# A hybrid DeltaNet/gMLP step: the first block begun behind two of four modulation quarters, their sums in column groups, x normed ahead of the halo rows

## The chip, the cores and the metric

The kernel runs on one core of a Trainium2 chip. The metric is device time in microseconds (us). Engines by their names in the profile: PE (TensorE matmul), PEld (its weight loads), DVE (VectorE), ACT (ScalarE), POOL (GpSimd) and SP, whose queue issues all DMAs of this kernel.

## The reference

One layer of a hybrid backbone for 128 context tokens and 2048 latent tokens of width 1024: an RMSNorm with a modulation computed from the conditioning vectors, a mixer (gated DeltaNet in two directions beside a gated spatial MLP, from one input projection), and a squared-ReLU MLP, each added to the residual.

```python
def modulation(cond, w_mod_l, b_mod_l):
    m = jax.nn.silu(cond) @ w_mod_l + b_mod_l
    return jnp.split(m[:, None, :], N_MOD, axis=-1)
...
    sh1, sc1, ga1, sh2, sc2, ga2 = mod
    h = rmsnorm(x, norm_mix_l) * (1.0 + sc1) + sh1
    o, s_new = mixer(h, s0, ...)
...
    proj = h @ w_in_l
    qkv = jax.nn.silu(centred_conv(qkv, conv_l))
```

Everything is float32. The change lies in the computation of `sh1` and `sc1`, of `h`, and of the first columns of `proj`, for the first 384 tokens.

## The kernel before

Tokens come as 17 tiles of 128 rows; tile 0 is the context. The first part works in six blocks, the first of tiles 0 to 2 (`BLOCKS`). For a block, `prep_block` makes eight *keys* `kH`, `kL` (one for each 128 of the 1024 features): features on partitions, tokens along the row, split in a rounded float32r part and its rest. In the first block a key is made from x normed by rows: three transposes on PE (a *turn*), the modulation by tables `a1`, `b1` on ACT into `full`, the split on DVE. A key has padding columns: zeros at the ends of a sequence, and *halo* columns, single neighbouring tokens needed by the convolution, which POOL casts from `halH` and `halL`; these come from ten halo rows `xh`, normed and transposed ahead. In the first block that is one column, 387.

`feature_tile` projects a block on 128 output features: for each key three matmuls (`mm3`: high by high, high by low, low by high), 24 in a group, into one PSUM buffer (`pj`, three of them, or `pt`), and then `convolve`, `to_tokens`, `to_features` and `products`. Group 1 (`gi` 1) are the k features, 0 the q, 2 the v, four tiles each. Weights come by 256 KB tiles (`raw_w`) and are split by `split_w`: a cast on ACT (`wH`), a difference on DVE (`wL`). `ab_block` projects the 16 gate columns.

The tables need four quarters of the modulation, each a product of the conditioning (two columns) with 1024 x 512 weights: m0 (shift, features 0 to 511), m1 (scale, the same features), m2 and m3 (shift and scale of features 512 to 1023). `mod_load` loads eight tiles, `mod_sum` sums them on PE in one row block of two partitions, `mod_out` transposes the row of sums and writes half a table. Keys 0 to 3 need m0 and m1, keys 4 to 7 also m2 and m3. The code issues m0, m1, m2, the halo rows, x, m3, the first four k weight tiles, and later twelve more; it emits the four sums ahead of the projections, in the order r0, r1, r2, r3. Then it runs keys 0 to 3 against three k feature tiles, makes keys 4 to 7, and goes on in the main loop, where each feature tile's steps are mixed with side work (`interleave`): weight splits of the next groups, modulation steps for the later parts of the layer (`MOD_STEPS` tells how many at each tile of the first block), the loads and keys of the next block.

Engine orders are made by a scheduler that simulates the program and takes, on each engine, what is ready first by order of emission, unless a dependence without a semaphore (`add_manual_dep` with `NoSync`) fixes the order. `WARM` is eight products of ones that PE runs at the very start. The pool `wp` has 49 places for tiles of 128 x 512, in which raw and split weights lie.

Of the kernel before, what the change touches and what calls it, by code (L numbers as in the profile page):

```python
# [8 lines left out]
F32 = mybir.dt.float32  # L9
# [31 lines left out]
MOD_STEPS = (1, 1, 0, 0, 0, 1, 0, 2, 0, 1, 1, 2)  # L41
# [23 lines left out]
def hybrid_step(  # L65
# [63 lines left out]
    def make_masks():  # L129

        one16 = wp.tile([P, P], F16, tag="w", name="one16")
        V.memset(one16, 1.0)
        bd = {}
        for w in (2, 4, 8, 16, 32, 64):
            m = bd2 if w == 2 else wp.tile([P, P], F16, tag="w", name=f"bd{w}")
# [159 lines left out]
    with ExitStack() as ph:  # L295
# [47 lines left out]

        def mod_load(half, c0):
            return [raw_w(w_mod[0, k * P : (k + 1) * P, c0 + half * 512 : c0 + half * 512 + 512])
                    for k in range(KT)]

        def mod_sum(raws, psum):

            pm = psum()  # L350
            for k in range(KT):
                T.matmul(pm[0:2, :], scond[:, k, :], raws[k], start=k == 0, stop=k == KT - 1)
            row = pf.tile([2, 512], F32, tag="first", name="first", bufs=2)
            A.copy(row, pm[0:2, :])
            return row

        def mod_out(row, half, dst, bias, scaled):

            pc = pm1()
            for i in range(4):  # L360
                T.transpose(pc[:, 2 * i : 2 * i + 2], row[:, i * P : (i + 1) * P], ident[0:2, 0:2])
# [9 lines left out]
        def split_mod_steps(jc):  # L371
# [3 lines left out]
            def fetch(k):  # L375
                u["raw", k] = pf.tile([P, 512], F32, tag="mraw", name="raw", bufs=2)
                load(out=u["raw", k], in_=w_mod[0, k * P : (k + 1) * P, jc * 512 : (jc + 1) * 512])

# [17 lines left out]

        m0 = mod_load(0, 0)
# [4 lines left out]
        r1 = mod_sum(m1, pj)  # L402
        m2 = mod_load(1, 0)
        mod_out(r0, 0, b1, vec[:, 0:8], False)

        make_masks()


        xh = pf.tile([P, D], F32, tag="xh", name="xh", bufs=1)[0:10, :]
        for m in range(5):  # L410
            load(out=xh[2 * m : 2 * m + 2, :], in_=x_sample[0, 255 + 384 * m : 257 + 384 * m, :])
        r2 = mod_sum(m2, pj)
# [8 lines left out]
        xs0 = []  # L421
        for t in BLOCKS[0]:
            x = p1.tile([P, D], F32, tag="x", name="x", bufs=3)
            load(out=x, in_=xrow(t))
            xs0.append(x)
        for x in xs0:
            norm_rows(x)

        def load_w1(gi, ks):
            return [w1_raw(gi, k) for k in ks]  # L430

        def w1_raw(gi, k):
            return raw_w(w_in[0, k * P : (k + 1) * P, gi * 512 : (gi + 1) * 512])
# [3 lines left out]
        def first_half(half):  # L437
            for k in range(half * 4, half * 4 + 4):
                V.tensor_scalar(out=hal[:, k, :], in0=hal[:, k, :], scalar1=a1[:, 1, k : k + 1],
                                scalar2=b1[:, 1, k : k + 1], op0=ALU.mult, op1=ALU.add)  # L440
            ks = slice(half * 4, half * 4 + 4)
            V.tensor_copy(halH[:, ks, :], hal[:, ks, :])
            V.tensor_tensor(out=halL[:, ks, :], in0=hal[:, ks, :], in1=f32(halH)[:, ks, :], op=ALU.subtract)

        def prep_block(bi):
# [49 lines left out]
            if bi == 0:  # L495
                zc, hc = [0, 129, 130], [(387, 1)]
            elif bi == 5:
                zc, hc = [n + 1], [(0, 8)]
            else:
                hc = [(0, 2 * bi - 2), (n + 1, 2 * bi + 1)]  # L500
            def column(k):
                full = p1.tile([P, 384], F32, tag="full", name="full", bufs=2)
                kH = p1.tile([P, 388], F32R, tag="h", name="kH", bufs=24)
                kL = p1.tile([P, 388], F32R, tag="h", name="kL", bufs=24)
# [6 lines left out]
                if bi == 0:  # L511
                    ps = pt()
                    for i, x in enumerate(xs):
                        T.transpose(ps[:, i * P : (i + 1) * P], x[:, k * P : (k + 1) * P], ident)
# [23 lines left out]
            blk = (hH, hL, ncol, segs)  # L538
# [5 lines left out]
        def feature_tile(blk, bi, gi, h):  # L544

            hH, hL, ncol, segs = blk
# [7 lines left out]
            def project(k):  # L554
                if k == 0:
                    u["ps"] = (pt if bi == 0 and j == 6 else pj)()
# [80 lines left out]
        def ab_block(blk, bi):  # L637
            hH, hL, ncol, segs = blk
# [3 lines left out]
            def project():  # L642
                ps = (pj if bi else pm1)()
                for k in range(KT):
                    T.matmul(ps[:, :ncol], abW[:, k, :], hH[k][:, :ncol], start=k == 0, stop=False)
                    T.matmul(ps[:, :ncol], abW[:, k, :], hL[k][:, :ncol], start=False, stop=k == KT - 1)
                for s, o, m, _ in segs:
# [116 lines left out]
        m3 = mod_load(1, D)  # L764
        wr = load_w1(1, range(4))
        mod_out(r1, 0, a1, vec[:, 8:16], True)
        r3 = mod_sum(m3, pm1)
        mod_out(r2, 1, b1, vec[:, 0:8], False)
        W1[1] += [split_w(r) for r in wr]
        first_half(0)  # L770
        abr = p1.tile([P, KT, 16], F32, tag="abr", name="abr", bufs=1)
        load(out=abr, in_=w_ab)
        wk = load_w1(1, range(4, KT))
        wr = load_w1(0, range(KT))
# [5 lines left out]
        mod_out(r3, 1, a1, vec[:, 8:16], True)  # L780
        W1[1] += [split_w(r) for r in wk]
        first_half(1)
        for k in range(4, KT):
            cols[k]()
        V.tensor_copy(abW[:, :, 0:16], abr)
        V.tensor_tensor(out=abW[:, :, 16:32], in0=abr, in1=f32(abW)[:, :, 0:16], op=ALU.subtract)
        wq = [lambda r=r: W1[0].append(split_w(r)) for r in wr]
        wv = [lambda k=k: W1[2].append(load_split(w_in[0, k * P : (k + 1) * P, 1024:1536])) for k in range(KT)]
# [3 lines left out]
        for bi in range(len(BLOCKS)):  # L792
            nxt = prep_block(bi + 1) if bi + 1 < len(BLOCKS) else None
            if bi == 0:
                order = [(1, 0), (1, 1), (1, 2), (0, 0), (0, 1), (1, 3), (0, 2), (0, 3)]
# [5 lines left out]
            for n, (gi, h) in enumerate(order):  # L801
                u = us[n] if bi == 0 and n < 3 else feature_tile(blk, bi, gi, h)
                tile_of[gi, h] = u
                main = u["main"][4:] if bi == 0 and n < 3 else u["main"]
# [1266 lines left out]
```

## Time and profile before

| what | us |
|---|---|
| runs | 2574.28, 2577.04, 2578.62 (median 2577.04) |
| profiled execution, its own time | 2580.59 |
| span of the profiled execution | 2578.7 |
| PE busy | 2539.4 |
| DVE busy | 1836.7 |
| ACT busy | 1259.7 |
| first projection matmul (line 241) | 36.20 |

In the lines of the profile a time stands in us from the span's start, followed by how long the row took, the engine, the line of the kernel, the operation, its output and inputs by the program's names, and in brackets the engine's idle time before it with what released it. A float32 matmul is two instructions there. Matmul ends are modelled, so starts are the better measure. The mean granted clock of the run is 0.997.

### The profile page before, as it was taken

What the parts mean: (1) busy time and instruction counts of PE and PEld (TensorE: products, weight loads), DVE (VectorE), ACT (ScalarE), POOL (GpSimd) and SP (SyncE); (2) the same over time, 40 slices, a digit from 0 to 9 for tenths busy, and PEclk for the clock granted to TensorE, in tenths of its full rate; (3) what the DMA queues carried; (4) which work ended last, traced back from release to release, by engine and by line L of the source; (5) the groups of instructions that cost most, each with busy time, mean ns of one, the idle gap of its engine ahead of it and who ended that gap; (6) DMA issues with size and microseconds to landing.
All of it is one profiled execution on the core that took longest, in us unless ns stands there. A gap on an engine that the chain in (4) does not pass through costs nothing.

```text
span 2578.7 us, 44496 instructions
## 1 busy us (share of the span) xinstructions
PE 2539.4 (98%) x15268; PEld 2139.2 (83%) x15268; DVE 1836.7 (71%) x3790; ACT 1259.7 (49%) x3119; POOL 234.2 (9%) x448
## 2 busy tenths in 40 slices
PE   9999999999999999999999999999999999999998
PEld 5999999788888787778888888888888888888887
DVE  5867757776677878886677876777675557685875
ACT  4755556555555667764355543544442433243442
POOL 3112212111111111210000000000000000000000
PEclk9999999999999999999999999999999999999999
DMA  8967737644454657885768789666579979786683
GB/s 293 307 209 216 209 111 256 225 158 153 145 156 159 214 165 243 277 274 176 281 204 257 231 270 358 194 181 188 148 248 370 331 273 330 259 259 205 221 264 113
DMA packets 503912, 588.66 MB, mean 228 GB/s; under 512 B 36148, under 2 KB 298588, under 8 KB 500102
## 3 DMA queue, kind: packets, MB, share of 16 engines
q1 hardware_dynamic: 503686, 585.82, 69.6%
q8 instruction: 120, 1.97, 0.3%
q14 instruction: 106, 0.87, 0.1%
HBM read 406.01 MB, written 179.67 MB: 227 GB/s over the span
## 4 chain that ended last, share of the span: by engine, by line
PE 89%; DMA 5%; DVE 4%; ACT 1%; issue 1%; POOL 0%; SPq 0%; POOLq 0%; DVEq 0%; ACTq 0%
PE f L241 17%; PE f L242 17%; PE f L243 17%; PE pj L241 7%; PE pj L243 7%; PE pj L242 7%; PE pd L1010 5%; PE pm L241 1%; PE pm L243 1%; PE pm L242 1%; DMA raw<-in_w_mod_dram 1%; PE pt L625 1%; PE pt L584 1%; PE pd L1093 1%; DMA hop_d<-opL 1%
## 5 line engine op out<-in xcount | busy, mean ns | idle before, releaser
L241 PE MATMUL f<-hop,zH 128*128 128x512 f32 (+1 forms) x976 | 376.2, 386 | 1.2 <-ACT zH L1531 1.2
L242 PE MATMUL f<-hop,zH 128*128 128x512 f32 (+1 forms) x976 | 376.1, 386 | 0.0
L243 PE MATMUL f<-hop,zL 128*128 128x512 f32 (+1 forms) x976 | 376.1, 386 | 0.0
L241 PE MATMUL f<-hop,wH 128*128 128x512 f32 x896 | 349.7, 391 | 0.6 <-ACT p L1604 0.6
L242 PE MATMUL f<-hop,wH 128*128 128x512 f32 x896 | 348.7, 389 | 0.0
L243 PE MATMUL f<-hop,wL 128*128 128x512 f32 x896 | 347.5, 389 | 0.0
L1531 ACT CAST zH<-zraw 128x512 fp32r<-128x512 f32 x240 | 146.9, 620 | 302.4 <-DMA zraw<-s_d 93.6
L241 PEld LDWEIGHTS f<-hop,zH 128*128 128x128 f32 x976 | 183.3, 188 | 38.6 <-ACT zH L1531 1.6
L243 PEld LDWEIGHTS f<-hop,zL 128*128 128x128 f32 x976 | 183.3, 188 | 37.3 <-DVE zL L1525 0.4
L242 PEld LDWEIGHTS f<-hop,zH 128*128 128x128 f32 x976 | 183.3, 188 | 36.9 <-issue 0.2
L1525 DVE TENSOR_TENSOR zL<-zraw,zH 128x512 fp32r<-128x512 f32 x240 | 163.2, 687 | 66.5 <-ACT zH L1531 54.0
L241 PEld LDWEIGHTS f<-hop,wH 128*128 128x128 f32 x896 | 168.2, 188 | 36.5 <-ACT p L1604 1.7
L243 PEld LDWEIGHTS f<-hop,wL 128*128 128x128 f32 x896 | 168.2, 188 | 35.3
L242 PEld LDWEIGHTS f<-hop,wH 128*128 128x128 f32 x896 | 168.3, 188 | 34.5
L241 PE MATMUL pj<-kH,wH 128*128 128x386 f32 (+2 forms) x568 | 190.5, 338 | 1.3 <-ACT junk L601 1.1
L243 PE MATMUL pj<-kH,wL 128*128 128x386 f32 (+2 forms) x568 | 189.7, 335 | 0.0
L242 PE MATMUL pj<-kL,wH 128*128 128x386 f32 (+2 forms) x568 | 189.5, 335 | 0.1
L184 POOL TENSOR_TENSOR r<-rsq,nhalf 128x1 f32<-128x1 f32 (+1 forms) x37 | 25.7, 694 | 1409.0 <-DVE rsq L183 1409.0
L571 DVE SCALAR_TENSOR_TENSOR cv<-pj,vec,cv 128x384 f32<-128x384 f32 (+2 forms) x164 | 87.0, 539 | 53.4 <-ACT cv L568 52.0
L1531 ACT CAST wH<-s 128x512 fp32r<-128x512 f32 x96 | 59.4, 621 | 124.6 <-DVE s L1525 118.3
L241 PEld LDWEIGHTS pj<-kH,wH 128*128 128x128 f32 x568 | 107.1, 189 | 4.4 <-issue 2.4
L202 DVE TENSOR_TENSOR wL<-raw,wH 128x512 fp32r<-128x512 f32 x120 | 81.7, 688 | 40.0 <-ACT wH L201 36.6
(418 smaller groups left out, 5806.9 us busy)
## 6 DMA issues: line engine op xcount, KB each, us to landing
zraw<-z_d SPq DMA_DIRECT2D x212, 256.0 KB
raw<-in_w_ff_dram SPq DMA_DIRECT2D x192, 256.0 KB
hop<-hop_d SPq DMA_DIRECT2D x28, 1024.0 KB
z_d<-c SPq DMA_DIRECT2D x96, 256.0 KB
zraw<-s_d SPq DMA_DIRECT2D x96, 256.0 KB
raw<-in_w_mod_dram SPq DMA_DIRECT2D x80, 256.0 KB
r<-in_w_ff_dram SPq DMA_DIRECT2D x80, 256.0 KB
s_d<-s SPq DMA_DIRECT2D x64, 256.0 KB
```

Source lines behind the costliest of these rows:

```text
L184: G.tensor_tensor(out=out, in0=t[:np_, :n], in1=nhalf[:np_, :n], op=ALU.pow)
L202: V.tensor_tensor(out=lo, in0=raw, in1=f32(h), op=ALU.subtract)
L241: T.matmul(ps, lh, rh, start=first and i == 0, stop=False, skip_group_check=more)
L242: T.matmul(ps, lh, rl, start=False, stop=False, skip_group_check=more)
L243: T.matmul(ps, ll, rh, start=False, stop=last and i == n - 1, skip_group_check=more)
L571: V.scalar_tensor_tensor(out=cv[:, o : o + m], in0=ps[:, s + sh : s + sh + m], scalar=convw[:, w, j : j + 1], in1=cv[:, o : o + m], op0=AL ...
L584: T.transpose(pq[:, i * P : (i + 1) * P], u["x2"][:, i * P : (i + 1) * P], ident)
L625: T.matmul(ps[:, i * P : (i + 1) * P], kTt[:, i * P : (i + 1) * P], rhs[:, i * P : (i + 1) * P], start=True, stop=True)
L1010: T.matmul(p[:, h, :], lhs[:, h, :], rhs[:, h, :], start=True, stop=True)
L1093: T.matmul(py[:, h], u["X"][:, h, :], pm[:, h], start=True, stop=True)
L1525: V.tensor_tensor(out=out, in0=a, in1=b, op=op)
L1531: A.copy(h, src)
```

## The change

- `mod_sum` sums the eight k-tiles in four column groups of PE: k goes to output partitions 32 x (k mod 4), with the conditioning padded to 32 columns (`scg`). The row copy takes all 128 partitions, and `mod_out` multiplies by a selector `sel` that adds the four groups, in place of the transposes.
- Loads are issued in one fixed order: halo rows (two DMAs in place of five), m0, columns, x, m1, four k weight tiles, m2, m3, four more, gate weights, eight q weight tiles.
- x is normed with one power for the three tiles. The masks and the zero columns of the keys are made ahead of it.
- Key 0 and 1 are turned ahead; the projections start behind m0 and m1 alone. Four k feature tiles (in place of three) run keys 0 to 5 before the main loop, with the sums of m2 and m3 placed ahead of keys 2 and 3.
- `keep_on` puts filler products of ones on PE at four places (8, 16 and 8 matmuls after the first sum, after the halo transposes and ahead of key 0).
- `own_order` fixes the order of PE, DVE and ACT over that stretch as it is emitted; `follow` puts other loads behind the last of the fixed ones.
- The fourth k tile comes fourth (it came sixth), the gate columns move from tiles 1 and 2 to 5 and 6 of the first block, and `MOD_STEPS` is shifted to later tiles, with the same total of nine.

```diff
-MOD_STEPS = (1, 1, 0, 0, 0, 1, 0, 2, 0, 1, 1, 2)
+MOD_STEPS = (0, 0, 0, 0, 0, 1, 1, 2, 1, 1, 1, 2)
...
+        scg = p1.tile([P, KT, 32], F32, tag="scg", name="scg", bufs=1)
+        V.memset(scg, 0.0)
+        V.tensor_copy(scg[:, :, 0:2], scond)
+        sel = p1.tile([P, 2], F32, tag="sel", name="sel", bufs=1)
+        V.tensor_tensor(out=sel, in0=ident[:, 0:2], in1=ident[:, 32:34], op=ALU.add)
+        for g in (64, 96):
+            V.tensor_tensor(out=sel, in0=sel, in1=ident[:, g : g + 2], op=ALU.add)
...
-                T.matmul(pm[0:2, :], scond[:, k, :], raws[k], start=k == 0, stop=k == KT - 1)
-            row = pf.tile([2, 512], F32, tag="first", name="first", bufs=2)
-            A.copy(row, pm[0:2, :])
+                g = 32 * (k % 4)
+                T.matmul(pm[g : g + 32], scg[:, k, :], raws[k], start=k < 4, stop=k >= 4)
+            row = pf.tile([P, 512], F32, tag="first", name="first", bufs=2)
+            A.copy(row, pm)
...
-                T.transpose(pc[:, 2 * i : 2 * i + 2], row[:, i * P : (i + 1) * P], ident[0:2, 0:2])
+                T.matmul(pc[:, 2 * i : 2 * i + 2], row[:, i * P : (i + 1) * P], sel, start=True, stop=True)
...
+        def own_order(start, *engines):
+            rows = tc.nc.cur_bb.bb.instructions
+            for e in engines:
+                own = [x for x in rows if x.engine == e]
+                at = len(own) - sum(x.engine == e for x in rows[start:])
+                for x, y in zip(own[max(at - 1, 0):], own[max(at, 1):]):
+                    tc.add_manual_dep(y, x.name, mybir.DependencyInfo(
+                        mybir.DependencyClass.NoSync, mybir.DependencyReason.DATA), reason="order")
+        def keep_on(n):
+            for _ in range(n):
+                T.matmul(warm[:, P : 2 * P], ones, ones, start=True, stop=True)
+        make_masks(pf.tile([P, 6, P], F16, tag="x2", name="one6", bufs=4))
+        edges = []
...
+        start = here()
+        xh = pf.tile([P, D], F32, tag="xh", name="xh", bufs=1)[0:10, :]
+        load(out=xh[0:8, :], in_=x_sample[0, 255 : 255 + 4 * 384, :].rearrange("(m r) d -> m r d", r=384)[:, 0:2, :])
+        load(out=xh[8:10, :], in_=x_sample[0, 255 + 384 * 4 : 257 + 384 * 4, :])
         m0 = mod_load(0, 0)
         load(out=vec, in_=v_columns)
         convw = vec[:, 32:68].rearrange("p (w a) -> p w a", w=3)
+        (loads of the three x tiles, xs0)
         m1 = mod_load(0, D)
+        w1a = load_w1(1, range(4))
+        m2 = mod_load(1, 0)
+        m3 = mod_load(1, D)
+        w1b = load_w1(1, range(4, KT))
+        (load of abr)
+        wr = load_w1(0, range(KT))
+        own_order(start, mybir.EngineType.SP)
+        loaded = tc.nc.cur_bb.bb.instructions[-1]
+        pinned = here()
         r0 = mod_sum(m0, pm1)
+        keep_on(WARM)
         norm_rows(xh)
...
+        mod_out(r0, 0, b1, vec[:, 0:8], False)
         V.tensor_copy(hal, ps[:, 0:80].rearrange("p (k j) -> p k j", k=KT))
+        keep_on(2 * WARM)
...
+        for i, x in enumerate(xs0):
+            A.activation(junk, x, AF.Square, accum_out=ss[:, i : i + 1])
+        rsqrt_cols(r, ss, 3, 1.0 / D, EPS)
+        for i, x in enumerate(xs0):
+            V.tensor_scalar_mul(x, x, r[:, i : i + 1])
+        r1 = mod_sum(m1, pj)
...
-                zc, hc = [0, 129, 130], [(387, 1)]
+                zc, hc = [], [(387, 1)]
...
-        us = [feature_tile(blk, 0, 1, h) for h in range(3)]
-        for k in range(4):
-            cols[k]()
-            for u in us:
+        us = [feature_tile(blk, 0, 1, h) for h in range(4)]
+        blk[4](0)
+        W1[1].append(split_w(w1a[0]))
         mod_out(r1, 0, a1, vec[:, 8:16], True)
+        first_half(0)
+        blk[4](1)
+        keep_on(WARM)
+        cols[0]()
+        cols[1]()
+        W1[1].append(split_w(w1a[1]))
+        for k in range(6):
+            if k == 2:
+                r2 = mod_sum(m2, pm1)
+            if k == 3:
+                r3 = mod_sum(m3, pm1)
+            for n, u in enumerate(us):
                 u["main"][k]()
+                if n == 1 and k == 2:
+                    mod_out(r2, 1, b1, vec[:, 0:8], False)
+                if n == 1 and k == 3:
+                    mod_out(r3, 1, a1, vec[:, 8:16], True)
+                    first_half(1)
+                    cols[4]()
+                    W1[1].append(split_w(w1b[0]))
+            if k < 2:
+                cols[k + 2]()
+                W1[1].append(split_w(w1a[k + 2]))
+            if k > 2:
+                cols[k + 2]()
+                W1[1].append(split_w(w1b[k - 2]))
+        own_order(pinned, mybir.EngineType.PE, mybir.EngineType.DVE, mybir.EngineType.Activation)
...
-                order = [(1, 0), (1, 1), (1, 2), (0, 0), (0, 1), (1, 3), (0, 2), (0, 3)]
+                order = [(1, 0), (1, 1), (1, 2), (1, 3), (0, 0), (0, 1), (0, 2), (0, 3)]
...
-                if n == 1:
+                if n == (1 if bi else 5):
                     ab1, ab2 = ab_block(blk, bi)
                     side.append(ab1)
-                if n == 2:
+                if n == (2 if bi else 6):
                     side.append(ab2)
```

`blk[4]` is the new function `turn` of `prep_block`: the three transposes of a key of the first block.

More of the change, by code (lines that the diff above doesn't have):

```diff
@@ L500, in prep_block, with turn @@
                 hc = [(0, 2 * bi - 2), (n + 1, 2 * bi + 1)]
+            turned = {}
+            def turn(k):
+                turned[k] = ps = pt()
+                for i, x in enumerate(xs0):
+                    T.transpose(ps[:, i * P : (i + 1) * P], x[:, k * P : (k + 1) * P], ident)
+                return ps
             def column(k):
                 full = p1.tile([P, 384], F32, tag="full", name="full", bufs=2)
[L503 to L504 removed]
+                if bi == 0:
+                    kH, kL = edges[k]
+                else:
+                    kH = p1.tile([P, 388], F32R, tag="h", name="kH", bufs=24)
+                    kL = p1.tile([P, 388], F32R, tag="h", name="kL", bufs=24)
                 for col in zc:
@@ L511, in column @@
                 if bi == 0:
-                    ps = pt()
-                    for i, x in enumerate(xs):
-                        T.transpose(ps[:, i * P : (i + 1) * P], x[:, k * P : (k + 1) * P], ident)
+                    ps = turned.pop(k) if k in turned else turn(k)
                     for s, o, m, cd in segs:
@@ L785, in hybrid_step, with third @@
+        own_order(pinned, mybir.EngineType.PE, mybir.EngineType.DVE, mybir.EngineType.Activation)
+        start = here()
         V.tensor_copy(abW[:, :, 0:16], abr)
         V.tensor_tensor(out=abW[:, :, 16:32], in0=abr, in1=f32(abW)[:, :, 0:16], op=ALU.subtract)
+        own_order(start, mybir.EngineType.DVE)
         wq = [lambda r=r: W1[0].append(split_w(r)) for r in wr]
-        wv = [lambda k=k: W1[2].append(load_split(w_in[0, k * P : (k + 1) * P, 1024:1536])) for k in range(KT)]
+        def third(k):
+            start = here()
+            raw = raw_w(w_in[0, k * P : (k + 1) * P, 1024:1536], sp, "raw")
+            follow(start, loaded, mybir.EngineType.SP)
+            W1[2].append(split_w(raw))
@@ L789, in hybrid_step @@
+        wv = [lambda k=k: third(k) for k in range(KT)]
         decay = decay_steps()
```

87 lines of the change are left out of this document (42 added, 45 removed).

## The prediction

> **What bounds the kernel now.** I read the page first, then the first 75 us in windows of 5 us, then the timelines of the engines there.
>
> ```profile
> span 2578.7 us, 44496 instructions
> PE 2539.4 (98%) x15268; PEld 2139.2 (83%) x15268; DVE 1836.7 (71%) x3790; ACT 1259.7 (49%) x3119; POOL 234.2 (9%) x448
> ```
>
> The span is TensorE's: only 39 us of it are not PE. So an edit of the start gains only by letting PE do its projections sooner, and what it gains stays, unless something later holds PE up. The profiled execution took 2580.59 us, 1.9 around its span; the runs shown have the median 2577.04. I work out a difference on the trace and take it from 2577.04. The runs lie 0.17% apart, so about 0.2%, 5.2 us, is what can be told from no change.
>
> The windows of the start (busy us of each engine, granted clock, DMA share, GB/s):
>
> ```profile
> core 0: us, PE busy (x) PEld busy (x) DVE busy (x) ACT busy (x) POOL busy (x), PEclk, DMA share, GB/s
> 0.00:5.00 5.00, 3.76 (x17) 3.49 (x18) 1.84 (x13) 1.50 (x2) 4.28 (x29) 1.00 0.55 161
> 5.00:10.00 5.00, 5.00 (x13) 0.89 (x12) 0.01 (x1) 0.00 (x0) 3.39 (x29) 1.00 0.97 325
> 10.00:15.00 5.00, 5.00 (x13) 0.97 (x12) 0.29 (x2) 0.58 (x1) 4.64 (x12) 1.00 1.05 390
> 15.00:20.00 5.00, 5.00 (x16) 1.17 (x15) 1.81 (x12) 0.57 (x1) 0.09 (x1) 1.00 1.05 386
> 20.00:25.00 5.00, 5.00 (x16) 1.12 (x15) 0.94 (x3) 2.30 (x4) 0.80 (x2) 1.00 0.90 292
> 25.00:30.00 5.00, 4.16 (x18) 1.19 (x16) 3.27 (x11) 2.76 (x5) 1.41 (x3) 1.00 1.02 391
> ```
>
> PE and the DMA engines are both full here. PE's rows, with the projections from 36.20 on and, of a stretch of 38 of them without a gap, the first and the last:
>
> ```profile
> 16.39 7.89 PE L352 MATMUL pj<-raw,scond 128*2 128x512 f32 x18
> ...
> 32.67 3.59 PE L352 MATMUL pm<-raw,scond 128*2 128x512 f32 x8
> 36.20 0.62 PE L241 MATMUL pj<-kH,wH 128*128 128x388 f32 x2
> ...
> 38.64 0.41 PE L361 MATMUL pm<-ident,first 2*128 2x2 f32 x4
> ...
> 57.61 0.34 PE L241 MATMUL pj<-kH,wH 128*128 128x388 f32 x1
> ...
> 64.14 0.34 PE L242 MATMUL pj<-kL,wH 128*128 128x388 f32 x1
> ```
>
> A sum is 8 k-tiles of two instructions. 18 of them take 7.89 us, the last 0.59 of it its own length, so one starts every 0.43 us and a sum costs 6.9 us; four sums (27.5 us) fill PE until 36.20. From there one projection matmul starts every 6.53/37 = 0.177 us.
>
> **The change, part by part.**
>
> *The new start.* What a first key needs ahead of it in SP's order: the conditioning vector, two DMAs of halo rows, m0, the columns, three x tiles and m1: 16 tiles of 0.262 MB, 1.57 of x and 0.08, 5.85 MB. By the windows 4.38 MB are moved at 15 us and 5.85 at 18.8. Two halo issues ahead cost 2 x 3.74/8 = 0.94 us of SP; landing lags behind moving:
>
> ```profile
> 1.25 3.74 SPq L190 DMA_DIRECT2D raw<-in_w_mod_dram  x8
> ...
> 27.38 1.06 ACT L335 ACTIVATE junk<-x 128x1024 bf16<-128x1024 f32 x1 [0.95 <-DMA x<-in_x_sample_dram]
> ```
>
> The third x tile closes 7.95 MB of issues (24 modulation tiles of 0.262 MB, 1.57 of x, small ones) and is there at 27.38, when 8.70 MB have moved: 1.9 us late at 390 GB/s. So m1 lands at 18.8 + 0.9 + 1.9 = 21.6. The chain behind it, with rows of the old one:
>
> ```profile
> 32.78 0.91 ACT L516 ACTIVATE full<-pt,b,a 128x128 f32<-128x128 f32 x2 [3.79 <-PE pt L514]
> ...
> 36.50 0.57 ACT L354 COPY first<-pm 2x512 f32<-2x512 f32 x1
> ```
>
> ```profile
> 33.27 0.25 DVE L519 CAST kH<-full 128x128 fp32r<-128x128 f32 x1 [2.28 <-ACT full L516]
> ...
> 34.09 0.42 DVE L520 TENSOR_TENSOR kL<-full,kH 128x256 fp32r<-128x256 f32 x1
> ...
> 39.84 0.23 DVE L368 SCALAR_TENSOR_TENSOR a<-a,vec 128x4 f32<-128x4 f32 x2
> ...
> 41.17 0.68 DVE L202 TENSOR_TENSOR wL<-raw,wH 128x512 fp32r<-128x512 f32 x1
> ```
>
> Last piece of the sum 0.9, row copy 0.6, four matmuls against the selector and their drain about 1.1 (four transposes took 0.41), table 0.6, then 1.3 from the first ACT piece to kH (1.7 to kL; 32.78 to 34.51). So projections start at about 26.1 instead of 36.2: **-10.1**. x is normed beside this: landed about 16.2, three squares, one power on POOL instead of three, three scalings, done near 20.6. The 32 filler matmuls (64 instructions of 0.11, 7 us) lie in PE's waits for m0, xh, m1 and the table. The extra weight padding, selector and masks run on DVE and POOL before 11 us, where DVE is busy 0.01 us in the window from 5. The zero edges are the same POOL casts, earlier.
>
> *The other two sums, now behind the start.* Their price in column groups is shown by the four-group sums later in this block:
>
> ```profile
> 149.62 0.62 PE L280 MATMUL pm<-acc,pick 128*2 128x128 f32 x16
> 150.17 0.44 PE L241 MATMUL pj<-kH,wH 128*128 128x386 f32 x1
> ```
>
> ```profile
> 116.11 1.34 PE pt L625 x12
> ```
>
> 12 full 128-column products take 1.34 us, 0.112 each; 16 in groups would be 1.79 in a row and took 0.55, so 3.25 at a time. 6.9/3.25 = 2.1 us a sum; perfect overlap gives 1.7, none 6.9. Two sums, at 1.85 between the overlap seen and the perfect one, since 512 columns hide the switch better than 128: **+3.7**. Their outputs now are products with 128-wide weights: 0.6 each by the row of 0.41 (bounds 0.4 and 1.3), and one of two lay behind 36.2 before: **+0.8**.
>
> *Key 4.* m2 lands at 29.7, m3 at 35.1 (5.4 us per 2.1 MB, behind m1 and four weight tiles at 390 GB/s). PE reaches the sum of m3 at 26.1 + 36 x 0.177 + two turns 0.5 + 1.85 + 0.6 = 35.4, so it hardly waits for the load. The sum ends near 37.3; then come two tiles' key 3, the output, and the table at 40. PE is out of key 3 at 40.6, kH of key 4 is there at 41.3, its wL (0.68 more) at 42.4, while PE needs that for its third matmul; keys 6 and 7 come about 0.8 late again, since each turn stands behind a key's twelve matmuls: 0.7 + 0.7 + 0.8, **+2.2**, bounds 0 (other tiles' matmuls fill it) and 4.
>
> *The halo column.* Each key also waits for two POOL casts, of halH and halL.
>
> ```profile
> 43.18 4.92 POOL L509 CAST kH<-halH 128x1 fp32r<-128x1 f32 x1
> 48.04 0.30 POOL L509 CAST kH<-halH 128x1 fp32r<-128x1 f32 x2
> ```
>
> ```profile
> 48.27 0.28 DVE L519 CAST kH<-full 128x128 fp32r<-128x128 f32 x1 [0.21 <-ACT full L516]
> ```
>
> One cast of a single column took 4.92 us and ended at DVE's first gap; the next pair took 0.30. That cost PE nothing because keys 0 to 3 of three tiles and the gate columns were still to do. Now PE stands at key 4 with nothing else allowed by the fixed order. DVE's work from the halo split to its next wait (the turn of key 6) is two keys of 1.25 and two wL of 0.6: POOL would get in near 44.3, and PE start key 4 then, 2.1 us after it otherwise would have it whole. I take half, **+1.0**, since the first cast of that group got through; bounds 0 and 2.1. The Trainium skill, *SBUF — State Buffer*, section *Who interferes with whom*, says that the pair of ports shared by DVE and GpSimd is locked for a whole instruction and the loser fully blocks. The row of 4.92 us agrees; by the rule alone the sum would have 2.1 here and give 2575.7.
>
> *What moves behind.* Gate columns go from the second to the sixth tile, the fourth key tile comes earlier, modulation steps go later with the same number (nine in the block). No instruction is added; priced 0. Cover: DVE idle at 60 to 65, which moves with it; bounds -1.9 and +6.7 (rivals).
>
> Sum: -10.1 + 3.7 + 0.8 + 2.2 + 1.0 = -2.4, so **2574.6**.
>
> **Rivals.**
>
> *More than the sum.* PE's waits before:
>
> ```profile
> 69.12 0.52 PE L584 MATMUL pt<-ident,x 128*128 128x128 f32 x3 [0.30 <-DVE ab L656]
> ...
> 70.96 0.52 PE L584 MATMUL pt<-ident,x 128*128 128x128 f32 x3 [0.44 <-DVE x L575]
> ...
> 72.61 0.41 PE L241 MATMUL pj<-kH,wH 128*128 128x388 f32 x1 [1.13 <-ACT junk L601]
> ```
>
> ```profile
> 65.03 1.06 ACT L467 ACTIVATE junk<-x 128x1024 bf16<-128x1024 f32 x1 [5.00 <-DMA x<-in_x_sample_dram]
> ```
>
> ACT sat 5 us in its queue on block 1's x, behind it the convolutions, and PE lost 1.9. If the loads bundled at the head let x come sooner, this goes; with the halo casts in gaps (-1.0) and other tiles in the wait at key 4 (-2.2) it is 2569.5; an m1 a microsecond sooner gives 2568.5. For it: SP's weight loads no longer mix with key stores. Against: SP still has 32 stores ahead of x.
>
> *Full lock of POOL.* All casts of the group wait for DVE's gap, as the second did for 4.92 us: +2.1 in place of +1.0, 2575.7. For it: the row itself; against: DVE may wait for ACT earlier than I have it. (It is what the rule cited above says.)
>
> *The start is paid back later.* DMA is at 1.02 of its engines in the windows by 25 to 30 us. If block 0 as a whole ends when its transfers do, the head is lost: 2577. Against: the 39 us that PE lacks in the whole span, which leave no long wait there.
>
> *x behind the stores (slower).* The stores of keys leave SP one by one:
>
> ```profile
> 54.09 0.43 SPq L534 DMA_DIRECT2D hH_d<-kH  x1
> ...
> 60.67 0.42 SPq L534 DMA_DIRECT2D hL_d<-kL  x1
> 61.19 0.45 SPq L462 DMA_DIRECT2D x<-in_x_sample_dram  x1
> ```
>
> 14 stores from 54.09 to 60.67 go every 0.51 us. If all 32 follow the last weight load near 43, x is issued at 59 and there at 63, while the first tile is convolved near 52 and PE, with the other tiles' buffers full, has work to about 55: 8.6 us of waiting instead of 1.9, +6.7, 2581.3, and with the full lock 2582.4. It decides once ACT takes the square of x ahead of the second tile's convolution and x is over 5 us late.
>
> *Sums that do not overlap (slower).* If groups with 32 columns and 512 moving columns run one after another, the edit does not do what it says: two sums at 6.9 add 2 x 5.05, 2584.7. Against it stands 0.55 us for 16.
>
> **How the numbers follow.** The forecast 0.34, full lock 0.12, paid back 0.08; more than the sum 0.30; x behind the stores 0.10 (0.06 of it over 0.2% slower); no overlap 0.06. The engine orders behind the fixed part are made anew, which may give or cost 3 us and puts 0.03 of the forecast on either side. So faster 0.33, same 0.28 + 0.12 + 0.08 + 0.04 = 0.52, slower 0.15. The range of eight in ten reaches from 2567, under the faster case, to 2582.5, over x behind the stores; the likeliest case's own is 2572 to 2577.5.
>
> **What would show it.** Right: the first projection between 24.5 and 28, sums of 16 instructions at about 2 us, a PE gap of 1 to 4 us before or within key 4's first matmuls, released by POOL or DVE. A gap of ACT on block 1's x over 6 us says x behind the stores. Wrong: projections after 30 (m1 later than worked out), sums of 6 us, or PE waits changed by more than 5 us in sum after 130, which none of these steps touches.

## The result, and the profile after

The changed kernel takes 2594.99 us (median of 6 runs, 2591.36 to 2596.70), the kernel before 2577.20 on the same chip: ratio 1.0069, 95% interval 1.0056 to 1.0082. It is 17.8 us slower, where 2.4 us less were forecast. The profiled execution took 2593.1 us, its span is 2591.3. Line numbers below are each kernel's own; in the changed one the projections still start at line 241.

PE's busy time in the whole span is 2.6 us less than before; the span grew by PE's waiting:

```profile
span 2591.3 us, 44604 instructions
PE 2536.8 (98%) x15348; PEld 2150.2 (83%) x15348; DVE 1837.7 (71%) x3789; ACT 1259.0 (49%) x3119; POOL 230.3 (9%) x430
```

PE's timeline of the changed kernel, from the first projection to the restart after a long gap (bracket: PE's idle time before the row, and what ended it):

```profile
28.55 0.42 PE L241 MATMUL pj<-kH,wH 128*128 128x388 f32 x1
...
33.92 1.92 PE L361 MATMUL pm<-raw,scg 128*32 128x512 f32 x16
36.95 0.95 PE L370 MATMUL pm<-sel,first 128*128 128x2 f32 x8
39.00 1.92 PE L361 MATMUL pm<-raw,scg 128*32 128x512 f32 x16
42.02 0.95 PE L370 MATMUL pm<-sel,first 128*128 128x2 f32 x8
45.18 0.41 PE L241 MATMUL pj<-kH,wH 128*128 128x388 f32 x1 [0.44 <-POOL kL L575]
...
54.85 0.34 PE L243 MATMUL pt<-kH,wL 128*128 128x388 f32 x1
69.44 0.66 PE L241 MATMUL pj<-kH,wH 128*128 128x388 f32 x1 [14.25 <-ACT junk L521]
...
72.48 0.53 PE L241 MATMUL pj<-kH,wH 128*128 128x388 f32 x1
72.81 0.38 PE L242 MATMUL pj<-kL,wH 128*128 128x388 f32 x1
73.03 0.34 PE L243 MATMUL pj<-kH,wL 128*128 128x388 f32 x1
```

Up to 54.85 the change does what it says: projections 7.65 us sooner than 36.20, two sums of 1.9 us among them, no stop over 0.44 us at key 4. Then four finished tiles hold their PSUM buffers, PE has nothing it may do in its order, and it stands 14.25 us. ACT and SP in the same stretch:

```profile
51.86 2.17 ACT L201 CAST wH<-raw 128x512 fp32r<-128x512 f32 x4
64.59 1.06 ACT L521 ACTIVATE junk<-x 128x1024 bf16<-128x1024 f32 x1 [10.56 <-DMA x<-in_x_sample_dram]
...
66.16 1.34 ACT L631 ACTIVATE cv<-pj,vec 128x128 f32<-128x128 f32 x4
```

```profile
43.22 0.33 SPq L597 DMA_DIRECT2D hH_d<-kH  x1
...
59.90 0.42 SPq L597 DMA_DIRECT2D hL_d<-kL  x1
60.41 0.44 SPq L516 DMA_DIRECT2D x<-in_x_sample_dram  x1
```

ACT finished its casts at 54.0 and next had the square of block 1's x in its queue; that x was issued at 60.41, behind nearly all of block 0's key stores, and ACT stood 10.56 us. The first convolution (line 631), which alone frees a buffer, is behind the square, at 66.16. ACT's 10.56 us and PE's 14.25 us are one wait. PE's row names ACT's second square, which ended just ahead of 69.44; but by the code the buffer is free only when DVE has read it too, and DVE's last piece of the first convolution, the first of the three in this row, ended at 69.29 after weight differences (`wL`) ahead of it:

```profile
68.81 1.13 DVE L634 SCALAR_TENSOR_TENSOR cv<-pj,vec,cv 128x256 f32<-128x256 f32 x3
```

The whole of it, from the first projection to the first matmul of the next part (`pm<-wH,hH`), in one window of each kernel (before, then after; columns as before: busy us of PE, PEld, DVE, ACT, POOL, granted clock, DMA share, GB/s):

```profile
36.20:400.80 364.60, 361.66 (x2314) 350.10 (x2314) 258.86 (x557) 213.61 (x639) 67.21 (x179) 1.00 0.70 211
```

```profile
28.55:415.90 387.35, 368.94 (x2353) 353.63 (x2354) 261.35 (x558) 215.00 (x641) 67.22 (x198) 0.98 0.69 205
```

The start gives 7.65. PE's idle time rises from 2.9 to 18.4: +15.5. Its busy time rises by 7.3: two sums 3.7 (spaced 1.85), 16 output instructions 0.1 apart in place of 4 transposes, about 1.3, the restart about 1.5 (below), and 0.8 spread. Sum +15.1, which is where the two traces stand apart at 400.8 (415.90). Behind that PE is busy just as long in both (2143.6 us) and idle 34.3 us before and 31.8 after, so the spans end 12.6 apart. The medians are 17.8 apart because the profiled execution of the kernel before took 3.4 us more than its median and that of the changed kernel 1.9 less.

### The profile page after: what moved, and what is told of

Same layout as the page of the kernel before. It is cut to its first block, busy times and chain, and to the rows that moved or that the text cites. A ratio compares the mean times of both kernels' runs of the same rounds, so it can differ in the third digit from the quotient of the medians.

```text
span 2591.3 us, 44604 instructions
## 1 busy us (share of the span) xinstructions
PE 2536.8 (98%) x15348; PEld 2150.2 (83%) x15348; DVE 1837.7 (71%) x3789; ACT 1259.0 (49%) x3119; POOL 230.3 (9%) x430
## 4 chain that ended last, share of the span: by engine, by line
PE 86%; DMA 6%; DVE 4%; ACT 1%; issue 1%; SPq 1%; POOL 0%; POOLq 0%; DVEq 0%; ACTq 0%
PE f L241 16%; PE f L243 16%; PE f L242 16%; PE pj L241 7%; PE pj L242 7%; PE pj L243 7%; PE pd L1095 5%; PE pm L241 1%; PE pm L243 1%; PE pm L242 1%; DMA raw<-in_w_mod_dram 1%; PE pt L688 1%; PE pt L647 1%; PE pd L1178 1%; DMA QK<-qk_d 1%
## 5 line engine op out<-in xcount | busy, mean ns | idle before, releaser
L241 PE MATMUL pj<-kH,wH 128*128 128x386 f32 (+2 forms) x568 | 191.9, 340 | 18.3 <-ACT junk L521 14.2
L184 POOL TENSOR_TENSOR r<-rsq,nhalf 128x1 f32<-128x1 f32 (+2 forms) x35 | 24.8, 708 | 1404.6 <-DVE rsq L183 1404.6
L241 PEld LDWEIGHTS pj<-kH,wH 128*128 128x128 f32 x568 | 107.7, 190 | 22.9 <-ACT junk L521 14.5
```

The costliest lines, as they stand in the source:

```text
L184: G.tensor_tensor(out=out, in0=t[:np_, :n], in1=nhalf[:np_, :n], op=ALU.pow)
L241: T.matmul(ps, lh, rh, start=first and i == 0, stop=False, skip_group_check=more)
```

## The experiments

Theory A: ACT, which takes its queue in order, stands on block 1's x, because the scheduler put the square ahead of the first convolution while the load is behind the stores on SP. Rival T: the transfers are late whatever the order. Rival G: the late gate columns leave PE without work.

"Offset" in the table is where a kernel's trace stands against the kernel before at the first `pm<-wH,hH` (400.77 there). "Idle" is the length from its first projection to there, less PE's busy time in a window of just that length. "Over before" is the median against that of the kernel before in the same batch, with the ratio's interval. One execution of each kernel was profiled; its clock alone moves the first projection by about 2 us (last section), so the offsets hold that much chance.

| kernel | first projection | idle | offset | over before, us | ratio |
|---|---|---|---|---|---|
| before | 36.20 | 2.9 | 0 | 0 | |
| changed | 28.55 | 18.4 | +15.1 | +17.8 | 1.0056 to 1.0082 |
| order_first | 28.60 | 11.1 | +9.8 | +12.4 | 1.0031 to 1.0064 |
| order_third | 29.06 | 7.7 | +6.4 | +7.1 | 1.0018 to 1.0041 |
| stores_late | 28.57 | 16.7 | +15.0 | +18.1 | 1.0061 to 1.0091 |
| x_early | 29.72 | 10.9 | +10.7 | +27.9 | 1.0092 to 1.0129 |
| x_first | 29.41 | 8.4 | +10.4 | +14.4 | 1.0044 to 1.0072 |
| x_first_gates | 26.86 | 6.9 | +2.1 | +4.2 | 1.0004 to 1.0024 |
| gates_back | 27.34 | 16.6 | +14.2 | +11.9 | 1.0028 to 1.0054 |
| groups_alone | 38.06 | 5.9 | +7.5 | +9.6 | 1.0018 to 1.0042 |
| all_three | 26.79 | 8.4 | +6.5 | +9.4 | 1.0023 to 1.0049 |
| all_three_pt | 28.93 | 13.2 | +16.5 | +19.4 | 1.0058 to 1.0086 |
| short_fill | 28.83 | 16.4 | +14.5 | +16.6 | 1.0052 to 1.0079 |
| no_filler | 27.10 | 18.6 | +18.5 | +19.8 | 1.0064 to 1.0093 |
| stores_spread | 27.22 | 5.5 | +1.8 | +5.5 | 1.0011 to 1.0030 |
| stores_spread_free | 28.86 | 4.7 | +1.7 | +5.2 | 1.0012 to 1.0033 |

**The order on ACT.** Two kernels fix the squares of block 1's x behind convolutions: `order_first` behind those of the first and second tile, `order_third` all three behind the third, with the steps after them one tile later.

```diff
+                start = here()
                 A.activation(junk, x, AF.Square, accum_out=xs[0][:, i : i + 1])
+                if bi == 1:
+                    follow(start, conv_act[-1], mybir.EngineType.Activation)
...
+                conv_act.append(tc.nc.cur_bb.bb.instructions[-1])     # ACT's last step of each convolution
```

order_first: 

> The changed kernel with one thing added: on ACT, the square of each x tile of block 1 stands behind the convolution of the first (second, second) k feature tile; nothing else is moved by hand. Theory A (ACT's order: the square of x waits for a load behind 32 key stores, ahead of every convolution, and holds all PSUM buffers): the first buffers come free, PE does one or two q feature tiles (4.2 us each) inside its wait of 14.25 us, which shrinks to 6 to 10; time 2586 to 2591. Theory B (block 0 ends when its transfers or DVE's work end, so a wait taken away here comes back later): PE's wait moves, time 2592 to 2597.

order_third: 

> The changed kernel, with the three squares of block 1's x placed behind the convolution of the third k feature tile on ACT; the steps behind them (column factors, rows, loads of transposed x) one feature tile later. Theory A: no PE wait over 3 us between 50 and 75 us, the granted clock there stays at 1.00, and 14.25 us of waiting and 1.5 of half clock go: 2577 to 2581. Theory B: 2590 to 2597, with the wait found again before 135 us.

Measured 2590.01 and 2584.72. PE and ACT of order_third:

```profile
55.24 0.37 ACT L646 ACTIVATE cv<-pj,vec 128x128 f32<-128x128 f32 x1 [0.68 <-PE pj L243]
```

```profile
59.94 0.66 PE L241 MATMUL pj<-kH,wH 128*128 128x388 f32 x1 [4.21 <-DVE cv L649]
73.63 0.80 PE L397 MATMUL pm<-wH,abW 128*128 128x512 f32 x1 [2.82 <-ACT wH L201]
```

The convolution now starts after 0.68 us of ACT's waiting for its tile, 10.9 us sooner, and PE's wait falls from 14.25 to 4.21, the length of a convolution among weight casts on ACT and DVE. So theory A holds for the large wait. order_first's time lies in A's range, with three waits on convolutions, 6.4 us together, in place of one. The time of order_third is 3.7 us above A's range and below B's: the 4.21 us are more than the 3 that A allowed, and a new wait stands at 73.63, behind ACT, which stood 6.62 us on a weight load.

**The load's place.** `stores_late` emits block 0's key stores only at tiles 2 to 5; `x_early` loads block 1's x in halves right behind the fixed weight loads.

```diff
+                def keep():                # stores_late: the stores of a key, called later
...
+                    late.append(keep)
...
+                    if bi == 0 and 2 <= n < 6:
+                        side += late[2 * n - 4 : 2 * n - 2]
...
+        xs1 = [[raw_w(xrow(t)[:, h * 512 : h * 512 + 512]) for h in range(2)] for t in BLOCKS[1]]   # x_early
```

stores_late: 

> The changed kernel, with the 32 stores of block 0's keys emitted at feature tiles 2 to 5 in place of with the keys, so that SP issues block 1's x first. ACT's order by the program is as in the changed kernel. Theory A: x is issued when its buffers come free, about 51 us, and there at 55; the square holds ACT 0 to 3 us, PE waits under 3 us; 2577 to 2582. Theory B, or that the weight casts and not x held ACT: PE waits over 8 us as before, 2590 to 2597.

x_early: 

> The changed kernel, with block 1's three x tiles (used for their squares alone) loaded in halves right behind the last fixed weight load; stores stay with the keys. Theory A: no wait for x; 2576 to 2580. If the head start is real (projections begun 7.6 us sooner) and nothing takes it back, this one is at or below the kernel before. Theory B: 2588 to 2597.

Measured 2595.76 and 2605.58; neither is in A's range. In stores_late, whose time lies in B's range, SP issued x at 59.77, 0.6 us sooner: later emission hardly moved the stores, 27 of which still went ahead of x, and PE stood 13.44 us in one wait. The edit did not do what it was for, so that run says nothing on the theories. In x_early the load was early, and ACT was held all the same, earlier:

```profile
43.81 0.63 ACT L526 ACTIVATE junk<-raw 128x512 bf16<-128x512 f32 x1 [6.07 <-DMA raw<-in_x_sample_dram]
```

```profile
48.07 1.87 PE L370 MATMUL pm<-sel,first 128*128 128x2 f32 x8 [4.72 <-ACT first L363]
```

The squares were taken ahead of the row copy of m3's sum, and PE waited 4.72 us for that instead. The same mechanism at another place. With no x in ACT's way behind the four tiles, PE's wait there was 4.20 us (at 66.38), as in order_third. The kernel loses still more behind 400 us (+10.7 there, +27.9 in time), which is not explained.

**x ahead of the stores.** `x_first` fixes the x loads ahead of the stores of keys 2 to 7; `x_first_gates` also puts the gate columns back at the second and third tile; `gates_back` does only that.

```diff
+        ahead = [i for i in ... if i.engine == mybir.EngineType.SP][-1]     # the last x load
+        for f in late:
+            f()
+        follow(start, ahead, mybir.EngineType.SP)
...
-                if n == (1 if bi else 5):      # x_first_gates, gates_back
+                if n == 1:
...
-                if n == (2 if bi else 6):
+                if n == 2:
```

x_first: 

> The changed kernel with the three loads of block 1's x put on SP ahead of block 0's key stores 2 to 7 (24 of the 32 stores then follow the loads). Theory A (ScalarE stands on block 1's x, which comes behind the stores): x is issued near 51 to 53 us, when the last key is turned, instead of 60.4 to 63.5, and is there by 57; TensorE's wait of 14.2 us near 69 shrinks to the 4.2 us that were left when the squares were moved behind the first convolutions, and the later loads come sooner too, so that no second wait of 2.7 us is left: 2581 to 2586. Rival T (it is the transfers themselves that are late, in whatever order): the waits only move, 2590 to 2596.

x_first_gates: 

> As x_first, and the gate columns of block 0 at the second tile again, as in the kernel before, instead of the sixth. Theory B (what remains of the wait is that four key tiles abreast end together, hold all buffers, and TensorE has nothing else to do until the first is convolved): 16 matmuls of 0.178 us fill 2.85 us of the 4.2, 2.5 to 3.5 us less than x_first: 2578 to 2583. If the gate columns do not matter: the same as x_first within 1 us.

gates_back: 

> The changed kernel with only the gate columns of block 0 back at the second tile. Theory A with B: ScalarE still stands on x, so the wait of 14.2 us loses just the 2.85 us of the 16 matmuls: 2591 to 2593. Rival G (the late gate columns are the main cause of the loss): 2578 to 2585.

Measured 2593.64, 2583.47 and 2591.16. gates_back's time came as A says, and PE still stood 13.16 us in one wait, so rival G falls. That it fits so well is in part luck: the wait lost 1.1 us where 2.85 were expected, and the first projection came 1.2 us sooner by the clock. x_first missed A's range by 7.6 us, and its time lies in rival T's; but x, issued at 51.63, was there at 55.16, and PE's wait went down to 3.38, so the transfer of x was not what was late. PE waited 2.84 us more at 79.0, where ACT had stood 4.46 us on a weight load, restarted below full clock twice, and its busy time was 4.4 us above the changed kernel's. x_first_gates is 10 us faster than x_first where 2.85 were expected; up to the next part the traces show 8.3 of it: 2.5 by an earlier first projection (by the clock, below), 1.5 less idle and 4.2 less busy time. So this is no measure of the gate columns alone. In x_first_gates ACT stood on x once more; x was issued at 50.39 and came 6.9 us later, against 3.5 in x_first, so rival T keeps a part of this wait; why the transfer took longer is not explained:

```profile
57.29 1.06 ACT L526 ACTIVATE junk<-x 128x1024 bf16<-128x1024 f32 x1 [5.46 <-DMA x<-in_x_sample_dram]
```

```profile
61.53 0.66 PE L241 MATMUL pj<-kH,wH 128*128 128x388 f32 x1 [5.17 <-DVE cv L644]
```

**All of it.** `all_three` adds the order of order_first to x_first_gates; `all_three_pt` gives the fifth tile a buffer of `pt` besides.

```diff
-                    u["ps"] = (pt if bi == 0 and j == 7 else pj)()
+                    u["ps"] = (pt if bi == 0 and j in (7, 0) else pj)()      # all_three_pt
```

all_three: 

> x_first_gates with the squares of block 1's x ordered on ScalarE behind the first convolutions, as in order_first. In x_first_gates ScalarE still stood 5.5 us on x (issued at 50.4, there at 57.3) ahead of the first convolution, and TensorE waited 5.2 us. Theory A (the order on ScalarE is the wait): the convolution starts when the first tile ends near 53, its buffer is free 4.2 us later, and with the gate columns until 56.2 TensorE waits about 1.2 us instead of 5.2; with 1 us less at half clock: 2577 to 2580. Rival (the convolutions are late for VectorE's and ScalarE's weight casts, whatever stands on x): a wait of 4 to 5 us stays, 2582 to 2585.

all_three_pt: 

> all_three, and the fifth tile gets one of the three buffers of the other group (pt), as the fourth tile does, so that its projections need no convolution first. Theory B (TensorE waits for a buffer): the last of the wait goes and TensorE's clock does not fall near 60; 1 to 3 us less than all_three, 2575 to 2578. If a buffer is not what it waits for (the fifth tile's weights, cast behind the convolutions): the same as all_three within 1 us.

Measured 2588.44 and 2598.42. The first wait of PE fell to 1.33 us as A said, and yet all_three's time is above both ranges, 5 us more than x_first_gates: ACT now stood on the next load that SP issues behind the stores.

```profile
57.62 0.42 PE L241 MATMUL pj<-kH,wH 128*128 128x388 f32 x1 [1.33 <-DVE cv L647]
...
74.44 0.87 PE L661 MATMUL pt<-ident,x 128*128 128x128 f32 x3 [2.72 <-DVE cv L647]
```

```profile
72.55 0.62 ACT L201 CAST wH<-raw 128x512 fp32r<-128x512 f32 x1 [6.71 <-DMA raw<-in_w_in_dram]
```

all_three_pt does not test the buffer. Its gap of 1.34 us stayed because the row at 59.79 again writes a `pj` buffer: the scheduler put the tile with the buffer of `pt` behind three others, at 83.0. The transposes waited 2.50 us at 76.39 and 2.58 at 80.75 (2.72 and 1.22 in all_three); that one `pt` fewer does this is not shown. Whether a free buffer would close the gap stays open.

**Spreading the stores.** `stores_spread` puts the stores of keys 2 to 7 behind the third weight group's first loads too, a key with each tile from the fifth to the tenth; `stores_spread_free` does it without the order on ACT.

```diff
+                if bi == 0 and 4 <= n <= 9:
+                    side.append(lambda f=late[n - 4]: keys_out(f))     # each behind SP's last load so far
```

stores_spread: 

> all_three, with the key stores 2 to 7 of block 0 behind not only block 1's x but also the first loads of the third weight group: two stores pairs with each of the fifth to tenth tile. In all_three ScalarE stood 6.7 us on such a weight load (there at 72.5, issued at 68.1 behind 24 stores), and TensorE then waited 2.7 and 1.2 us and ran at half clock near 75. Theory S (whatever ScalarE needs next and SP issues behind the stores becomes the next wait): that wait of ScalarE falls under 2 us, TensorE's idle time from the first projection to 400 us falls from 8.2 to 4 us or less, 2579 to 2584 instead of 2588.4. Rival (the transfers or the casts behind them limit this stretch, the order of SP does not): idle time stays at 6 to 8 us, 2586 to 2590.

stores_spread_free: 

> The same spread of the stores on x_first_gates, that is without the order of the squares on ScalarE. Theory S: TensorE's 5.2 us at the first convolution stay, since ScalarE stands on x there, and the rest is as in stores_spread: 3 to 5 us slower than stores_spread. If the order of the squares does not matter once x comes early: within 1.5 us of it.

Measured 2582.75 and 2582.49. The window of stores_spread:

```profile
27.20:402.60 375.40, 369.87 (x2354) 351.90 (x2355) 262.56 (x558) 215.44 (x641) 67.17 (x198) 1.00 0.70 213
```

Idle time fell from 8.4 in all_three to 5.5 and 4.7, above the 4 that theory S gave, and the time came as it said; ACT's wait on that weight load is 2.14 us, in place of 6.71. So the later waits were in the main the same thing again, loads behind stores. The order on ACT no longer matters once they are away: its expected 3 to 5 us did not show. With PE's waits nearly gone the trace of stores_spread stands at +1.8: the start gives 9.0, against 8.2 of busy time and 2.6 of idle. Of the busy time the two sums and the outputs are 5.0; the other 3.2 are not placed. By the intervals neither kernel can be told from x_first_gates, and none of the kernels beats the kernel before.

**Parts of the change.** `groups_alone` is the kernel before with just the sums in column groups and the selector; `no_filler` and `short_fill` are the changed kernel without fillers, and with 16 in place of 32 ahead of m1's sum.

```diff
-        keep_on(2 * WARM)
+        keep_on(WARM)          # short_fill
```

groups_alone: 

> The kernel before with only the sums in column groups, the selector and the wider rows; every order as before. If the sums alone held the projections up, the first projection comes when block 0's x is normed, near 32 us instead of 36.2, and the four tiles abreast and the late gate columns are not there: 2571 to 2575. If x and the halo rows, not the sums, set that start, or TensorE's clock drops because it idles between the short sums: 2575 to 2579.

no_filler: 

> The changed kernel without any filler product. Theory F (the fillers keep the granted clock up): the windows from 10 to 30 us show 0.5 to 0.7, the sum of m1 and the first projections run at half speed, 1 to 4 us slower, 2596 to 2599. If the fillers only stand ahead of the sum: the first projection 1 to 2.5 us sooner, 2592.5 to 2594.

short_fill: 

> The changed kernel with 16 instead of 32 filler products ahead of m1's sum. In the profile of the changed kernel these 32 took 5.45 us at a granted clock of 0.83 and the sum of m1 started right behind them; in x_first_gates they took 3.82 us at 1.00 and the first projection came 1.7 us sooner. If m1 is there before the fillers end: the first projection 1 to 2.5 us sooner, 2592.5 to 2594. If not, or if the clock falls further: the same or up to 2 us slower.

Measured 2588.87, 2598.86 and 2595.63. groups_alone makes the sums short, is slower than the kernel before, and lies 10 us above both of its ranges: PE, no longer filled by sums, lost its clock (window from 25 us), its projections began at 38.06, and the halo casts then held it:

```profile
25.00:30.00 5.00, 2.44 (x5) 0.46 (x4) 3.30 (x12) 2.30 (x4) 1.90 (x7) 0.50 1.00 373
30.00:35.00 5.00, 5.00 (x16) 2.34 (x15) 0.48 (x2) 0.00 (x0) 2.62 (x20) 0.50 1.06 384
```

```profile
46.32 8.22 POOL L518 CAST kH<-halH 128x1 fp32r<-128x1 f32 x4 [13.70 <-DVE halH L451]
```

```profile
54.23 0.62 PE L241 MATMUL pj<-kH,wH 128*128 128x388 f32 x2 [3.65 <-POOL kH L518]
```

no_filler is 3.9 us slower than the changed kernel by the medians, 2.0 by the differences to the kernel before of each batch, which is within the intervals. Its first projection came 1.5 us sooner, as the other theory had it, but its granted clock is lower than the changed kernel's 0.83:

```profile
20.00:25.00 5.00, 5.00 (x26) 2.24 (x21) 2.75 (x5) 1.10 (x2) 0.00 (x0) 0.63 1.05 387
25.00:30.00 5.00, 3.17 (x12) 2.79 (x11) 3.84 (x17) 2.23 (x5) 3.88 (x22) 0.71 1.06 388
```

So theory F holds for the clock: the fillers keep it up. In the mean over 15 to 25 us it is 0.66 here, against 0.83 or 1.00 in the twelve kernels with all fillers. What they are worth in time is not shown. short_fill changed nothing that can be told: with 16 fillers fewer the clock fell to 0.62 in the window from 20 us, and the first projection came at 28.83.

## Why the prediction was wrong

The step that failed is *What moves behind*, priced 0 with "Cover: DVE idle at 60 to 65" and bounds of -1.9 and +6.7. It came to 15.5 us of idle time and 1.5 of slow restart. I looked at the number of instructions and at DVE; what moved was the order of two waits on ACT. In the kernel before ACT also stood on block 1's x, but it had taken the first convolution 8 us ahead of the square at 65.03 (ACT of the kernel before); in the changed kernel the convolution lies behind the square.

The convolution in the kernel before:

```profile
56.93 1.36 ACT L568 ACTIVATE cv<-pj,vec 128x128 f32<-128x128 f32 x4 [3.70 <-PE pj L243]
```

The other steps and the rivals:

- *New start*, -10.1: measured -7.65. Where the granted clock stayed at 1.00 from 15 to 25 us (x_first_gates, all_three, stores_spread, gates_back) the same instructions start at 26.8 to 27.3, near the 26.1 worked out; where its mean there was 0.83, at 28.55 to 29.7. The step was right to about 1 us; the clock, which I took as 1, is the rest.
- *Two sums*, +3.7: 2 x 1.85, exact. *Outputs*, +0.8: 1.3, since eight instructions 0.1 us apart make an output 0.8 long where I had 0.6.
- *Key 4*, +2.2, and *halo column*, +1.0: the waits released by POOL and DVE near 45 are under 1 us together. Both were over-priced: POOL's eight casts ran from 44.19 to 46.14, beside rows of DVE with four pauses of 0.03 us between them.
- *x behind the stores*, a rival at 0.10 and 2581.3: this is what happened, with the marker that I had named, ACT standing over 6 us on x (10.56). Its place and cause were right; its price, 8.6 us of waiting, and its condition were wrong. I let it decide on the second tile's convolution; it decided on the first, which is the one that frees any buffer at all. With x at 63 as I had it, 1.6 us for the square and a cast, and 3.3 from the convolution's start to PE's restart (66.16 to 69.44), the wait would have been 63 + 4.9 - 55 = 12.9; x came at 64.59, and it is 14.25. Its chance was also too low: the stores, the order of issue and PE's end of work near 55 all stood in my text, and for ACT taking the convolution first I had only its order in the kernel before, where tiles end at other times.
- *More than the sum* needed x sooner; *sums that do not overlap* falls by 1.85 us a sum. *The start is paid back later* is not settled: even in stores_spread, with its waits nearly gone, the 9.0 us of the start went into busy time and small waits. *Full lock of POOL* did not show in the changed kernel, but does in groups_alone (8.22 us for four casts, 7.86 of it the first). The Trainium skill, *SBUF — State Buffer*, section *Who interferes with whom*, has the pair locked for an instruction at a time; here POOL stayed out over DVE's whole run of back-to-back instructions, 46.6 to 54.1, and came in at its end. That run has no pause; the small pauses are the difference that the traces show, and no run tests it.
- "PE waits changed by more than 5 us after 130" was right not to happen: from 130 to the next part PE waits 0.8 us in the changed kernel and not at all before, and behind that 2.5 us less. One wait of 2.72 us stands at 128.7.

## What to carry to other kernels

When a change makes more tiles finish together, look on the engine that drains them for what stands at the head of its queue at that moment, and on the DMA queue for what is issued ahead of the data it waits for; price the wait from the arrival of that data plus one drain, and not from busy time. An order that a scheduler makes anew is part of the change: fix the two or three places that free buffers, since emitting later (stores_late) hardly changed the order at all, and loading earlier (x_early) only moved the wait. Where several loads stand behind the same stores, look at all of them: in order_third, x_first and all_three the first load mended exposed the next, and spreading the stores took PE's idle time lowest, though not the time below x_first_gates.

## What the runs showed of the hardware

After the gap of 14.25 us PE ran at half speed: ten matmuls from 69.44, 0.32 to 0.33 us apart (the first 0.46), then 0.18 from 73.03 on: 3.4 us that cost about 1.5. The windows of the changed kernel:

```profile
55.00:60.00 5.00, 0.19 (x2) 0.00 (x0) 0.51 (x1) 0.00 (x0) 0.00 (x0) 0.92 0.67 196
60.00:65.00 5.00, 0.00 (x0) 0.00 (x0) 0.00 (x0) 0.41 (x1) 0.00 (x0) 0.50 0.93 240
65.00:70.00 5.00, 0.56 (x2) 0.59 (x3) 3.68 (x10) 4.78 (x12) 0.00 (x0) 0.50 0.84 291
70.00:75.00 5.00, 5.00 (x23) 5.00 (x22) 4.59 (x10) 5.00 (x13) 0.00 (x0) 0.71 0.53 157
```

The Trainium skill, *TensorE: Matmul & The Clock Gate*, section *What's actually happening*, gives half rate after an idle window of about 3.4 us and full rate after as long a stretch of work; both agree here. But the clock also fell where PE was never idle so long (its longest pause from 8 to 25 us is 1.32 us, ahead of 15.70): in the changed kernel it was 0.83 from 15 to 25 us,

```profile
15.00:20.00 5.00, 4.30 (x34) 4.28 (x35) 2.28 (x6) 2.54 (x6) 0.87 (x1) 0.83 1.06 388
20.00:25.00 5.00, 4.98 (x35) 3.18 (x34) 0.87 (x2) 0.36 (x1) 0.00 (x0) 0.83 1.05 385
```

and the 32 fillers there took 5.45 us where they take 3.82 at a clock of 1.00 (changed kernel, then x_first_gates):

```profile
17.20 5.45 PE L434 MATMUL pt<-ones 128*128 128x128 f32 x32
```

```profile
17.14 3.82 PE L434 MATMUL pt<-ones 128*128 128x128 f32 x32
```

The 0.83 is a mean, and no steady slower state: from 18.3 to 21.7 us the clock is 0.50, and on either side of it 1.00. In that stretch 16 of the fillers start 0.213 us apart, the others 0.112. Half speed for 3.4 us, as long as behind the gap, gives 0.83 over these 10 us and costs the 1.6 us. Of the twelve kernels with all fillers four have 1.00 in the mean over 15 to 25 us and eight 0.83, one such stretch; short_fill and no_filler have 0.66, two of them. What brings the stretch in one execution and not in another stays open.

The sum of m1 starts right behind the fillers in both, so in the changed kernel the fillers that are to keep the clock, slowed themselves, held the first projection back by 1.6 us.
